# A second buffer for raw MLP weights, a later MLP residual, and attention's residual made ahead of the scan

## The chip, the cores and the metric

The kernel runs on one core of one Trainium2 chip. The metric is the device time of one execution in microseconds (us); a lower time is better. The core has TensorE (PE in the profile, with its weight loads as PEld), VectorE (DVE), ScalarE (ACT), GpSimd (POOL) and SyncE (SP, which here only issues transfers).

## What is computed

One encoder layer over 1024 tokens of width 1024, in float32. The input is normalised, projected, and split into two head groups: four heads of a bidirectional gated DeltaNet (a chunked scan) and eight heads of neighbourhood attention. Their outputs are mixed by one projection; residual and LayerNorm follow, then a squared-ReLU MLP with residual and LayerNorm.

```python
x = layer_norm(x, ln_in_g, ln_in_b)
h = x @ w_in
o_gdn = gdn_mixer(...)                      # scan, both directions
o_na = rms_norm(neighborhood_attention(...))
mix = concat(o_gdn, o_na) @ w_out
x = layer_norm(ALPHA * x + mix, ln1_g, ln1_b)
ff = relu(x @ w1 + b1) ** 2
x = layer_norm(ALPHA * x + ff @ w2 + b2, ln2_g, ln2_b)
```

## The kernel before, in words

**Precision.** Every large operand is split into a high and a low part of type float32r: ScalarE copies the high part, and `sub_split` (line 71) subtracts it on another engine for the low part. A product takes three matmuls for each 128-row block.

**Order of work.** The program is written in Tile. A planner reads the whole program, allots the buffers of each tag, and puts every engine's instructions, and SP's and ACT's transfers, into one fixed order per engine: of the instructions whose inputs and buffers its own simulation holds to be ready, the one that comes first in the program goes first. So a transfer may be issued well ahead of its place in the text, as soon as its buffer is free. `tc.issue_after(ins)` holds an instruction behind another one, and `pacer` spreads matmuls of one kind behind anchors of another. On the chip each engine then works through its list in order, and an instruction that waits holds up all that stand behind it.

**Stages, in order of time.**
- Projection, convolution and the triangular inverse of the DeltaNet (lines 173 to 512), up to about 330 us. `inverse(b)` (lines 296 to 391) is one long chain on DVE (lines 311 to 317), a round trip through DRAM, and small matmuls with copies on ACT and DVE. The pool `p1` (from line 196) holds, among others, the tags `hraw` (2 buffers) and `cy` (3 buffers) of the convolution.
- The scan (lines 543 to 614), with the matmuls of attention's projections (`na_v`, `na_qk`) as filler between its steps. Its pool `p2` takes over space of `p1`, tile by tile.
- Attention (lines 719 to 765) in four passes `p` of two heads, 16 tiles of scores each, with parts of the output projection as filler: `units[p]` (line 820) says which. `out_proj` (line 792) splits its left side on ACT and POOL, multiplies, and adds two 128x512 halves into `yacc[t]` on DVE (line 805). Units 0 to 7 are the DeltaNet half for the eight 128-token blocks t; units 8 to 15 are the first half of attention's heads; the rest follows after pass 3.
- The residual of attention is made in pass 0 (lines 816 to 831). Two broadcasts `xg`, `xb` of ln_in_g and ln_in_b are loaded and scaled by ALPHA on ACT; each block of x is loaded into `yacc[t]`, normalised on ACT, and multiplied and added on POOL:

```python
                with tc.issue_after(loads[2 + t // 4].ins):
                    D.dma_start(yacc[t], A["x"][t * P:(t + 1) * P, :])
                S.activation(yacc[t], yacc[t], AF.Identity, scale=rstd0[:, t:t + 1], bias=nmr0[:, t:t + 1])
                G.tensor_tensor(yacc[t], yacc[t], xg, ALU.mult)
                G.tensor_tensor(yacc[t], yacc[t], xb, ALU.add)
```

- POOL also makes the small `rsqrt` of attention (line 93, from line 763) and the low part `ol` of `out_proj`. DVE makes the row sums for it with three tiny 128x4 instructions (lines 760 to 762).
- The MLP's first layer (lines 853 to 1178) uses Strassen's seven products in place of eight for 16 groups `g`: `w_steps` makes sums of w1 in tiles `ws` (tag `tt`, 6 buffers, shared with six early weight tiles `w1q`), `up_pair` multiplies. Between them `w2_load` and `w2_sums` (lines 1023 to 1036) read w2 in pieces of 256 KB a transfer into `w2r` (one buffer) and store sums for the second layer in DRAM (`t_d`).
- The MLP's second layer (lines 1145 to 1299) runs 7 products x 4 groups, n = 0 to 27. `down_ops(n)` loads two raw operands (1 MB each, into `big` or `q8` buffers) and splits them on ACT and DVE; `down_ops(n + 2)` is called ahead of n's matmuls. `first_ops` (line 1171) calls it for n = 0 and 1 in the last `up_pair`. `take(0, ...)` after n = 3 is the first to need the MLP's residual `yr`. That is made ahead of the loop (lines 1183 to 1194): five broadcasts, eight loads of `y_d`, and 18 DVE instructions.

Of the kernel before, what the change touches and what calls it, by code (L numbers as in the profile page):

```python
# [7 lines left out]
F32 = mybir.dt.float32  # L8
F32R = mybir.dt.float32r
AF = mybir.ActivationFunctionType  # L10
ALU = mybir.AluOpType
# [4 lines left out]
P = 128  # L16
T = 1024
DM = 1024
NK = DM // P
NT = T // P  # L20
DFF = 4096
NF = DFF // P
ALPHA = 2.0 ** 0.25
# [13 lines left out]
def tile_trunk(ctx: ExitStack, tc: tile.TileContext, A: dict, out: bass.AP):  # L37
    nc = tc.nc
    V, S, G, TE, D = nc.vector, nc.scalar, nc.gpsimd, nc.tensor, nc.sync
# [35 lines left out]
    dr = open_pool("dram", space=DRAM)  # L75
# [13 lines left out]
    rstd0 = cp.tile([P, NT], F32, name="rstd0")  # L89
# [128 lines left out]
    vt_d = dr.tile([8, P, 4, P], F32, name="vt_d")  # L218
    qk_d = [dr.tile([8, P, 4, P], F32, name=f"qk_d{d}") for d in range(2)]
    z_d = dr.tile([4, P, T], F32, name="z_d")  # L220
    gc_d = dr.tile([2, 2, 32, P], F32, name="gc_d")

    AY = [bigp.tile([P, 32, P], F32, tag="big", name=f"AY{b}", bufs=2) for b in range(2)]
# [287 lines left out]
        gdn_chunk("v", h)  # L511
    inverse(0)
    inverse(1)

    rk = p1.tile([P, 32], F32, name="rk")
    rkp = p1.tile([P, 32], F32, name="rkp")
# [196 lines left out]
    loads = []  # L713
# [75 lines left out]
    def raw8():  # L789
        return op.tile([P, 2, DM], F32, tag="q8", name="wraw", bufs=2)  # L790

    def out_proj(t, oT, hi, lo, pool, tag, eng, pace=lambda mm: None, nb=2):
        nk = len(hi)
        oh = pool.tile([P, nk, P], F32R, tag="oh", name="oh", bufs=nb)
        ol = pool.tile([P, nk, P], F32R, tag="ol", name="ol", bufs=nb)
        S.activation(oh, oT, AF.Copy)
        sub_split(eng, ol, oT, oh)
        for half in range(2):
            c = slice(half * 512, half * 512 + 512)
            ps = psC.tile([P, 512], F32, tag=tag[half % len(tag)], name="psop", bufs=2)  # L800
            for k in range(nk):
                pace(TE.matmul(ps, oh[:, k], hi[k][:, c], start=(k == 0), stop=False))  # L802
                pace(TE.matmul(ps, oh[:, k], lo[k][:, c], start=False, stop=False))
                pace(TE.matmul(ps, ol[:, k], hi[k][:, c], start=False, stop=(k == nk - 1)))
            V.tensor_tensor(yacc[t][:, c], yacc[t][:, c], ps, ALU.add)

    pre["h", 0] = load_qk(0)
    pre["b", 0, 0] = load_b(0, 0)
# [4 lines left out]
    with tc.issue_after(kload[0].ins):  # L813
        pre["v", 1] = load_v(1)
    wo1 = None
    xg, xb = (p3.tile([P, DM], F32, name=x) for x in ("xg", "xb"))
    for t_, nm in ((xg, "ln_in_g"), (xb, "ln_in_b")):
        D.dma_start(t_, A[nm].to_broadcast([P, DM]))
        S.activation(t_, t_, AF.Copy, scale=ALPHA)
    units = ((0, 1, 2, 3), (4, 5), (6, 7, 8, 9), range(10, 16))  # L820
    first = (2, 0, 0, 0)
    late = (0, 0, 0, 24)
    for p in range(4):
        attention(p)
        if p == 0:
            for t in range(NT):
                with tc.issue_after(loads[2 + t // 4].ins):
                    D.dma_start(yacc[t], A["x"][t * P:(t + 1) * P, :])
                S.activation(yacc[t], yacc[t], AF.Identity, scale=rstd0[:, t:t + 1], bias=nmr0[:, t:t + 1])
                G.tensor_tensor(yacc[t], yacc[t], xg, ALU.mult)  # L830
                G.tensor_tensor(yacc[t], yacc[t], xb, ALU.add)
        anchors = tiles[p * 16 + first[p]:p * 16 + 16]
        nmm = sum(24 if u < 8 else 12 for u in units[p]) - late[p]
        pace = pacer(anchors, 0, nmm / len(anchors), True)
        for u in units[p]:
            if u == 8:
                r = [raw8() for i in range(2)]
                wo1 = load_wo(1, [r[k // 2][:, k % 2] for k in range(4)])
            t = u % 8
            if u < 8:  # L840
                out_proj(t, oaccs[t // 4][:, t % 4], *wo0, p3, "p", G, pace)
            else:
                out_proj(t, oTn[0][:, :, t * P:(t + 1) * P], wo1[0][0:2], wo1[1][0:2], p3, "p", G, pace)
        attention_out(p)
# [22 lines left out]
        X[nm] = bigp.tile([P, 2, 4, 512], F32R, tag="big", name="x" + nm, bufs=2)  # L867

    def tmp(name):
        return wk.tile([P, 512], F32, tag="tt", name=name, bufs=6)  # L870

    def hold8(name):
        return wk.tile([P, 512], F32, tag="f0", name=name, bufs=8)
# [147 lines left out]
    raws1[1] = w1_raw(1)  # L1021

    def w2_load(g, hc):
        r = w2p.tile([P, 2, 2, 256], F32, tag="r", name="w2r", bufs=1)
        for k in range(2):
            D.dma_start(r[:, k], A["w2"][(2 * g + k) * P:(2 * g + k + 1) * P, :]
                        .rearrange("p (j c) -> p j c", j=2)[:, :, hc * 256:hc * 256 + 256])
        return r
# [152 lines left out]

    fp = open_pool("fin")
    gB, bB, g2B, b2L, b2B = (fp.tile([P, DM], F32, name=x) for x in ("gB", "bB", "g2B", "b2L", "b2B"))
    for t_, nm in ((gB, "ln1_g"), (bB, "ln1_b"), (b2B, "b2"), (g2B, "ln2_g"), (b2L, "ln2_b")):
        D.dma_start(t_, A[nm].to_broadcast([P, DM]))
    V.tensor_scalar(gB, gB, ALPHA, None, ALU.mult)
    V.scalar_tensor_tensor(bB, bB, ALPHA, b2B, ALU.mult, ALU.add)
    yr = []
    for t in range(NT):
        y = yp.tile([P, DM], F32, tag="y", name="yr", bufs=8)  # L1190
        D.dma_start(y, y_d[t])
        V.tensor_tensor(y, y, gB, ALU.mult)
        V.tensor_tensor(y, y, bB, ALU.add)
        yr.append(y)
    us = [fp.tile([P, 512], F32, name=f"us{q}") for q in range(4)]
    sts = {}

# [73 lines left out]
    for i in range(7):  # L1271
# [7 lines left out]
        for gr in range(NQ):  # L1279
            n = i * NQ + gr  # L1280
            if n + 2 < 7 * NQ:
                down_ops(n + 2)
            if i == 6 and gr >= NQ - 2:
                continue
            for q in range(4):
# [96 lines left out]
```

## Time and profile before

| what | value |
|---|---|
| time, median of 3 runs | 1384.3 us |
| lowest and highest of the runs | 1372.8 and 1384.89 us |
| the profiled execution's own time | 1387.8 us |
| span in its profile (first to last instruction) | 1385.8 us |
| mean granted TensorE clock | 0.977 |
| bytes moved by transfers | 268.32 MB |

The profile is of one execution. The span is what its rows divide; 2.0 us of the execution's time lie outside. The engines' busy shares are means over stages with different limits. In the rows, "[x <-E L]" is how long the engine had been idle ahead of an instruction and which instruction of which engine ended that; "x8" after a name is a count.

### The profile page before, as it was taken

The numbers are of one execution on the slowest core, as the hardware profiler recorded it, in microseconds if no ns is written. First come the engines' busy times: TensorE is split into PE (matmuls) and PEld (weight loads), VectorE is DVE, ScalarE is ACT, GpSimd is POOL, SyncE is SP. The second block draws the span as 40 slices with busy tenths as digits, with TensorE's granted clock in tenths as the row PEclk, the third lists the DMA queues.
The fourth block names the chain that finished last, engine by engine and source line by source line (L and its number), as shares of the span: only waits on it lengthen the run. The fifth ranks groups of instructions, "written<-read, shape, count | busy, mean of one in ns | idle before, by whom it ended". The sixth has DMA issues, their size and how long they took to land. (4 is left out here: it accounts for less than half of the span.)

```text
span 1385.8 us, 20027 instructions
## 1 busy us (share of the span) xinstructions
PE 1293.7 (93%) x7318; PEld 1072.5 (77%) x7318; DVE 947.9 (68%) x1707; ACT 634.3 (46%) x1224; POOL 187.8 (14%) x208
## 2 busy tenths in 40 slices
PE   5999999999999977699998899999998999999996
PEld 4688888888888866688875687777786788888885
DVE  6755797942348645757699886777875686565855
ACT  5457666434333145346366454444444433333531
POOL 3000001011113237513130000000000000000403
PEclk9999999999999999899999899999999899999998
DMA  6134548466877599565154677677779957555721
GB/s 193 51 99 126 145 122 182 124 147 202 234 224 222 135 277 329 150 173 147 45 179 134 213 257 250 208 248 259 238 267 354 396 197 246 182 182 193 257 96 61
DMA packets 242690, 268.32 MB, mean 194 GB/s; under 512 B 38928, under 2 KB 171920, under 8 KB 242592
## 3 DMA queue, kind: packets, MB, share of 16 engines
q1 hardware_dynamic: 208416, 216.70, 51.8%
q10 hardware_dynamic: 34176, 50.34, 10.4%
q8 instruction: 58, 0.95, 0.3%
q14 instruction: 40, 0.33, 0.1%
HBM read 181.99 MB, written 85.00 MB: 193 GB/s over the span
## 5 line engine op out<-in xcount | busy, mean ns | idle before, releaser
L1266 PE MATMUL psdn<-d,d 128*128 128x512 f32 (+1 forms) x464 | 175.3, 386 | 6.9 <-ACT d L1166 6.9
L1267 PE MATMUL psdn<-d,d 128*128 128x512 f32 (+1 forms) x464 | 177.9, 384 | 0.1
L1268 PE MATMUL psdn<-d,d 128*128 128x512 f32 (+1 forms) x464 | 177.6, 383 | 0.0
L71 DVE TENSOR_TENSOR d<-d2r,d 128x1024 fp32r<-128x1024 f32 x72 | 85.6, 1239 | 63.4 <-ACT d L1166 63.4
L1166 ACT ACTIVATE d<-d2r 128x1024 fp32r<-128x1024 f32 x72 | 71.3, 1048 | 109.5 <-PE psdn L1268 91.1
L1266 PEld LDWEIGHTS psdn<-d,d 128*128 128x128 f32 x464 | 88.0, 190 | 24.7 <-ACT d L1166 7.8
L1267 PEld LDWEIGHTS psdn<-d,d 128*128 128x128 f32 x464 | 87.8, 189 | 17.7 <-DVE d L71 0.6
L1268 PEld LDWEIGHTS psdn<-d,d 128*128 128x128 f32 x464 | 87.8, 189 | 17.2
L93 POOL TENSOR_TENSOR lrs<-lrs,mhalf 128x1 f32<-128x1 f32 x8 | 6.4, 806 | 615.5 <-DVE lrs L1208 615.5
L120 PE MATMUL psj<-xlo,whi 128*128 128x512 f32 x192 | 77.4, 403 | 1.9 <-DVE xlo L71 1.9
L119 PE MATMUL psj<-xhi,whi 128*128 128x512 f32 x192 | 77.0, 402 | 0.7 <-DVE xhi L170 0.7
L121 PE MATMUL psj<-xhi,wlo 128*128 128x512 f32 x192 | 76.5, 398 | 0.0
L71 DVE TENSOR_TENSOR d<-wraw,d 128x1024 fp32r<-128x1024 f32 x40 | 47.9, 1236 | 30.1 <-ACT d L1166 30.1
L1039 ACT ACTIVATE h<-h,b1T 128x512 f32<-128x512 f32 x48 | 34.7, 722 | 73.9 <-DVE h L1105 37.6
L71 DVE TENSOR_TENSOR wlo<-wraw,whi 128x1024 fp32r<-128x1024 f32 x28 | 34.3, 1223 | 47.9 <-ACT whi L110 43.3
L883 ACT ACTIVATE w1t<-ws 128x512 fp32r<-128x512 f32 x64 | 39.9, 626 | 57.9 <-DVE hs L1137 17.0
L1166 ACT ACTIVATE d<-wraw 128x1024 fp32r<-128x1024 f32 x40 | 40.0, 1049 | 55.1 <-PE psdn L1268 44.9
L240 DVE SCALAR_TENSOR_TENSOR cy<-hraw,convw,cy 128x1024 f32<-128x1024 f32 x48 | 61.2, 1281 | 5.6 <-ACT cy L238 4.5
L754 PEld LDWEIGHTS po<-vt,et 128*128 128x128 f32 x384 | 51.3, 194 | 7.9 <-ACT et L752 3.7
L743 ACT ACTIVATE ex<-sn,nm 128x384 f32<-128x384 f32 x64 | 39.0, 610 | 36.0 <-DVE nm L739 20.5
L754 PE MATMUL po<-vt,et 128*128 128x64 f32 x384 | 50.7, 271 | 4.4 <-ACT et L752 2.9
L802 PE MATMUL psop<-wo,oh 128*128 128x512 f32 x128 | 52.9, 416 | 1.6 <-ACT wo L785 1.3
(340 smaller groups left out, 3488.8 us busy)
## 6 DMA issues: line engine op xcount, KB each, us to landing
wraw<-in_w_dram SPq DMA_DIRECT2D x21, 1024.0 KB, 7.3
d2r<-h_d SPq DMA_DIRECT2D x18, 1024.0 KB, 5.5
w2r<-in_w_dram SPq DMA_DIRECT2D x64, 256.0 KB, 4.8
t_d<-w2s ACTq DMA_DIRECT2D x32, 512.0 KB, 4.8
h_d<-hs ACTq DMA_DIRECT2D x64, 256.0 KB, 2.1
wraw<-in_w_in_dram SPq DMA_DIRECT2D x28, 512.0 KB, 4.5
h_d<-h ACTq DMA_DIRECT2D x48, 256.0 KB, 5.3
d2r<-t_d SPq DMA_DIRECT2D x11, 1024.0 KB, 9.3
```

The source lines that it names most:

```text
L71: return eng.tensor_tensor(lo, full, f32(hi), ALU.subtract)
L119: pace(TE.matmul(ps, hi[:, kt], xhi[:, kt, sl], start=(kt == 0), stop=False))
L120: pace(TE.matmul(ps, hi[:, kt], xlo[:, kt, sl], start=False, stop=False))
L121: pace(TE.matmul(ps, lo[:, kt], xhi[:, kt, sl], start=False, stop=(kt == NK - 1)))
L240: V.scalar_tensor_tensor(y, raw[:, i:i + T], convw[:, ci, i:i + 1], y, ALU.mult, ALU.add)
L754: mm = TE.matmul(po[:, j], et[:, c], vts[j][:, t + c, e * 64:e * 64 + 64], start=(c == 0), stop=(c == 2))
L802: pace(TE.matmul(ps, oh[:, k], hi[k][:, c], start=(k == 0), stop=False))
L883: S.activation(t[:, 0], src, AF.Copy)
L1166: S.activation(t[:, 0, k], raw[:, k], AF.Copy)
L1266: TE.matmul(ps, h[:, 0, k, qs_], w[:, 0, k, c], start=(start and k == 0), stop=False)
L1267: TE.matmul(ps, h[:, 0, k, qs_], w[:, 1, k, c], start=False, stop=False)
L1268: TE.matmul(ps, h[:, 1, k, qs_], w[:, 0, k, c], start=False, stop=(stop and k == 3))
```

## The change

1. Attention's residual is made after the two `inverse` calls and ahead of the scan, in tiles of the tags `hraw` (`xg`, `xb`) and `cy` (`xs`): load, normalise on ACT, multiply and add on DVE, store to a DRAM tile `xr_d`. In attention the first `out_proj` of each block writes `yacc[t]` by two ACT copies instead of adding on DVE, and a transfer issued by POOL adds `xr_d[t]` to it in place.
2. `w2r` has two buffers; the tag `tt` has four instead of six.
3. The MLP's residual is made from n = 1 of the second layer's loop, behind the call of `down_ops(3)`, with three broadcasts; the other two (`g2B`, `b2L`) are loaded at n = 8. Its tiles `yr` are still allotted ahead of the loop.

```diff
+    xr_d = dr.tile([NT, P, DM], F32, name="xr_d")
...
     inverse(1)
+    xg, xb = (p1.tile([P, T + 4], F32, tag="hraw", name="xgb", bufs=2)[:, 0:DM] for i in range(2))
+    for t_, nm in ((xg, "ln_in_g"), (xb, "ln_in_b")):
+        D.dma_start(t_, A[nm].to_broadcast([P, DM]))
+        S.activation(t_, t_, AF.Copy, scale=ALPHA)
+    for t in range(NT):
+        xs = p1.tile([P, T], F32, tag="cy", name="xs", bufs=3)
+        D.dma_start(xs, A["x"][t * P:(t + 1) * P, :])
+        S.activation(xs, xs, AF.Identity, scale=rstd0[:, t:t + 1], bias=nmr0[:, t:t + 1])
+        V.tensor_tensor(xs, xs, xg, ALU.mult)
+        V.tensor_tensor(xs, xs, xb, ALU.add)
+        D.dma_start(xr_d[t], xs)
...
-            V.tensor_tensor(yacc[t][:, c], yacc[t][:, c], ps, ALU.add)
+            if first:
+                S.activation(yacc[t][:, c], ps, AF.Copy)
+            else:
+                V.tensor_tensor(yacc[t][:, c], yacc[t][:, c], ps, ALU.add)
...
-    xg, xb = (p3.tile([P, DM], F32, name=x) for x in ("xg", "xb"))
-    for t_, nm in ((xg, "ln_in_g"), (xb, "ln_in_b")):
-        D.dma_start(t_, A[nm].to_broadcast([P, DM]))
-        S.activation(t_, t_, AF.Copy, scale=ALPHA)
...
-        if p == 0:
-            for t in range(NT):
-                with tc.issue_after(loads[2 + t // 4].ins):
-                    D.dma_start(yacc[t], A["x"][t * P:(t + 1) * P, :])
-                S.activation(yacc[t], yacc[t], AF.Identity, scale=rstd0[:, t:t + 1], bias=nmr0[:, t:t + 1])
-                G.tensor_tensor(yacc[t], yacc[t], xg, ALU.mult)
-                G.tensor_tensor(yacc[t], yacc[t], xb, ALU.add)
...
-                out_proj(t, oaccs[t // 4][:, t % 4], *wo0, p3, "p", G, pace)
+                out_proj(t, oaccs[t // 4][:, t % 4], *wo0, p3, "p", G, pace, first=True)
+                G.dma_start(yacc[t], xr_d[t], accum_op=ALU.add)
...
-        return wk.tile([P, 512], F32, tag="tt", name=name, bufs=6)
+        return wk.tile([P, 512], F32, tag="tt", name=name, bufs=4)
...
-        r = w2p.tile([P, 2, 2, 256], F32, tag="r", name="w2r", bufs=1)
+        r = w2p.tile([P, 2, 2, 256], F32, tag="r", name="w2r", bufs=2)
...
-    for t_, nm in ((gB, "ln1_g"), (bB, "ln1_b"), (b2B, "b2"), (g2B, "ln2_g"), (b2L, "ln2_b")):
-        D.dma_start(t_, A[nm].to_broadcast([P, DM]))
...
-    for t in range(NT):
-        y = yp.tile([P, DM], F32, tag="y", name="yr", bufs=8)
-        D.dma_start(y, y_d[t])
...
+    yr = [yp.tile([P, DM], F32, tag="y", name="yr", bufs=8) for t in range(NT)]
+    def residual():
+        for t_, nm in ((gB, "ln1_g"), (bB, "ln1_b"), (b2B, "b2")):
+            D.dma_start(t_, A[nm].to_broadcast([P, DM]))
+        V.tensor_scalar(gB, gB, ALPHA, None, ALU.mult)
+        V.scalar_tensor_tensor(bB, bB, ALPHA, b2B, ALU.mult, ALU.add)
+        for t, y in enumerate(yr):
+            D.dma_start(y, y_d[t])
+            V.tensor_tensor(y, y, gB, ALU.mult)
+            V.tensor_tensor(y, y, bB, ALU.add)
...
             if n + 2 < 7 * NQ:
                 down_ops(n + 2)
+            if n == 1:
+                residual()
+            if n == 8:
+                for t_, nm in ((g2B, "ln2_g"), (b2L, "ln2_b")):
+                    D.dma_start(t_, A[nm].to_broadcast([P, DM]))
```

## Rows read from the trace of the kernel before

**Rows 1.** The page: busy time by engine, and PE's in 40 slices.

```profile
PE 1293.7 (93%) x7318; PEld 1072.5 (77%) x7318; DVE 947.9 (68%) x1707; ACT 634.3 (46%) x1224; POOL 187.8 (14%) x208
PE   5999999999999977699998899999998999999996
```

**Rows 2.** Stretches of 20 us: busy PE, PEld, DVE, ACT, POOL, PEclk, DMA share, GB/s.

```profile
500.00:520.00 20.00, 12.65 (x78) 10.33 (x76) 9.45 (x17) 8.92 (x18) 8.92 (x5) 1.00 1.01 276
520.00:540.00 20.00, 12.94 (x77) 11.91 (x78) 12.62 (x26) 16.54 (x30) 10.82 (x5) 0.83 1.03 360
540.00:560.00 20.00, 12.94 (x65) 10.28 (x64) 13.58 (x10) 3.13 (x6) 20.00 (x10) 0.91 0.98 243
560.00:580.00 20.00, 14.63 (x78) 12.71 (x79) 16.68 (x33) 8.35 (x24) 11.94 (x8) 0.75 0.39 108
580.00:600.00 20.00, 20.00 (x134) 18.24 (x133) 9.12 (x27) 7.71 (x19) 3.58 (x3) 1.00 0.56 161
```

**Rows 3.** Timeline of PE in the first attention pass.

```profile
524.56 0.69 PE L735 MATMUL pss<-kk,qs 128*128 128x384 f32 x1 [7.26 <-DVE nm L739]
...
564.54 0.69 PE L735 MATMUL pss<-kk,qs 128*128 128x384 f32 x1 [10.79 <-DVE nm L739]
```

**Rows 4.** DVE's groups by form, 500 to 580 us: busy us, mean ns.

```profile
L762 DVE SCALAR_TENSOR_TENSOR rs<-rs,sums 128x4 f32<-128x4 f32 x5 | 12.9, 2584 | 0.1
...
L761 DVE TENSOR_SCALAR sums<-sums 128x4 f32<-128x4 f32 x5 | 8.8, 1754 | 0.1
L760 DVE TENSOR_TENSOR sums<-sums 128x4 f32<-128x4 f32 x5 | 6.2, 1245 | 1.6 <-ACT ex L743 1.6
```

**Rows 5.** Timeline of DVE in the same pass.

```profile
523.94 0.56 DVE L739 CUSTOM_DVE_ANT_0 sn<-pss,B 128x384 f32<-128x384 f32 x1 [5.35 <-DMA B<-in_rpbT_dram]
...
552.71 11.30 DVE L762 SCALAR_TENSOR_TENSOR rs<-rs,sums 128x4 f32<-128x4 f32 x1
...
577.29 0.16 DVE L761 TENSOR_SCALAR sums<-sums 128x4 f32<-128x4 f32 x1
```

**Rows 6.** Timeline of POOL beside it.

```profile
551.23 4.65 POOL L830 TENSOR_TENSOR yacc<-yacc,xg 128x1024 f32<-128x1024 f32 x2
```

**Rows 7.** The tile yacc: durations min/median/max in ns, first and last start.

```profile
L828 SPq DMA_DIRECT2D yacc<-in_x_dram x8: 327/400/1116, 517.8 to 525.4; - x8
L829 ACT ACTIVATE yacc<-yacc,nmr,rstd x8: 1230/1236/1247, 527.9 to 539.8; 128x1024 f32<-128x1024 f32 x8
L830 POOL TENSOR_TENSOR yacc<-yacc,xg x8: 2331/2370/2391, 529.2 to 553.5; 128x1024 f32<-128x1024 f32 x8
L831 POOL TENSOR_TENSOR yacc<-yacc,xb x8: 2331/2353/2406, 533.8 to 569.4; 128x1024 f32<-128x1024 f32 x8
```

**Rows 8.** Timeline of SP's issues ahead of pass 0's second head.

```profile
513.95 2.30 SPq L818 DMA_DIRECT2D xg<-in_ln_in_g_dram  x1
...
516.82 0.91 SPq L709 DMA_DIRECT2D B<-in_rpbT_dram  x2
```

**Rows 9.** One stretch around the second inverse, columns as in rows 2.

```profile
255.00:335.00 80.00, 76.82 (x1261) 64.42 (x1260) 41.68 (x81) 30.77 (x50) 12.21 (x19) 0.96 0.61 149
```

**Rows 10.** The page's groups: a 128x1024 two-input DVE instruction.

```profile
L71 DVE TENSOR_TENSOR wlo<-wraw,whi 128x1024 fp32r<-128x1024 f32 x28 | 34.3, 1223 | 47.9 <-ACT whi L110 43.3
```

**Rows 11.** ACT's groups by form, 1100 to 1120 us: a 128x512 PSUM copy.

```profile
L1241 ACT ACTIVATE us<-psdn 128x512 f32<-128x512 f32 x4 | 2.4, 594 | 4.0 <-PE psdn L1268 4.0
```

**Rows 12.** Waits in the first MLP layer, 784 to 1060 us: total, times, longest.

```profile
PE psF L925 <- DVE u L1101: 9.0, 9, 2.1
...
DVE w2s L1032 <- DMA w2r<-in_w_dram: 14.2, 11, 2.7
```

**Rows 13.** Between the MLP's layers: SP's timeline.

```profile
1043.02 9.51 SPq L1191 DMA_DIRECT2D yr<-y_d  x5
...
1058.83 0.42 SPq L1163 DMA_DIRECT2D d2r<-h_d  x1
```

**Rows 14.** Between the MLP's layers: PE's timeline.

```profile
1075.89 2.07 PE L1266 MATMUL psdn<-d,d 128*128 128x512 f32 x4 [6.67 <-ACT d L1166]
```

More of the change, by code (lines that the diff above doesn't have):

```diff
@@ L790, in raw8, with out_proj @@
         return op.tile([P, 2, DM], F32, tag="q8", name="wraw", bufs=2)
-    def out_proj(t, oT, hi, lo, pool, tag, eng, pace=lambda mm: None, nb=2):
+    def out_proj(t, oT, hi, lo, pool, tag, eng, pace=lambda mm: None, nb=2, first=False):
         nk = len(hi)
@@ L1183, in tile_trunk @@
     gB, bB, g2B, b2L, b2B = (fp.tile([P, DM], F32, name=x) for x in ("gB", "bB", "g2B", "b2L", "b2B"))
-    for t_, nm in ((gB, "ln1_g"), (bB, "ln1_b"), (b2B, "b2"), (g2B, "ln2_g"), (b2L, "ln2_b")):
-        D.dma_start(t_, A[nm].to_broadcast([P, DM]))
-    V.tensor_scalar(gB, gB, ALPHA, None, ALU.mult)
-    V.scalar_tensor_tensor(bB, bB, ALPHA, b2B, ALU.mult, ALU.add)
-    yr = []
-    for t in range(NT):
-        y = yp.tile([P, DM], F32, tag="y", name="yr", bufs=8)
-        D.dma_start(y, y_d[t])
-        V.tensor_tensor(y, y, gB, ALU.mult)
-        V.tensor_tensor(y, y, bB, ALU.add)
-        yr.append(y)
+    yr = [yp.tile([P, DM], F32, tag="y", name="yr", bufs=8) for t in range(NT)]
[8 more added lines that the diff above has]
+            V.tensor_tensor(y, y, bB, ALU.add)
     us = [fp.tile([P, 512], F32, name=f"us{q}") for q in range(4)]
```

## The prediction

> **What bounds the kernel now.** I read the page first: PE is busy for 93% of the span [rows 1], so most of the kernel is matmul time that this change does not touch, and the most that any edit can win is PE's idle time and the time spent at a lower clock. The 40 slices say where that is: three slices stand at 7, 7 and 6 tenths in the middle, where attention starts, and single 8s stand in and behind the MLP's first layer [rows 1]. So I cut the middle into stretches of 20 us. From 500 to 580 us PE is busy 12.65 + 12.94 + 12.94 + 14.63 = 53.16 of 80 us, 26.8 us idle, with a granted clock of 0.83, 0.91 and 0.75 in the last three; the stretch behind it is full again [rows 2]. The transfers' share is about 1 for the first three, and POOL is busy for all of 540 to 560 [rows 2].
>
> PE's timeline there has two long gaps, 7.26 and 10.79 us, both ended by line 739 on DVE [rows 3]. DVE's timeline tells them apart. In the first, DVE itself waited for a bias tile B [rows 5]. In the second it waited for nothing: a 128x4 instruction of line 762 lasted 11.30 us [rows 5], while POOL ran its two-input instructions back to back [rows 6]. It is not a single accident: in this stretch the three tiny instructions of lines 760 to 762, 15 in all, took 6.2 + 8.8 + 12.9 = 27.9 us [rows 4]; one that nothing disturbs takes 0.16 [rows 5]. So some 27.9 - 15 x 0.16 = 25.5 us of DVE are lost to POOL's residual pass, whose 16 instructions of about 2.36 us [rows 7] make 37.8 us of POOL.
>
> The Trainium skill has a rule for this (page "SBUF — State Buffer", section "SBUF: two separate sides"): DVE with two SBUF inputs and GpSimd share one port pair, an exclusive lock held for one instruction. By that rule alone a tiny instruction would wait for one POOL instruction, 2.4 us, and the second gap would be some 2 us. The trace has 11.30, across several POOL instructions in a row, and I go by that.
>
> **The change, part by part.** The sum is made against the profiled execution, 1387.8 us. It lies 3.5 us above the median of the runs, 1384.3, and I take those 3.5 off at the end.
>
> *Attention, what goes.* The 16 POOL instructions, 8 ACT instructions of 1.236 us, 8 loads of x (4.2 MB) and the two broadcasts leave the stretch [rows 7, 8].
> - The gap of 10.79 us [rows 3] has no other cause in sight: -10.8.
> - The gap of 7.26 [rows 3] ends with B. B's issue at 516.82 stands right behind the two broadcasts, whose issues begin at 513.95 [rows 8]: 2.9 us earlier. B is not the only transfer under way, so I take -3 of the 7.26, between 0 and -7.
> - The rest of the 26.8 us idle, 8.8, is made of waits of about a us. The other blocked DVE instructions (25.5 - 11.1 = 14.4 us of DVE) are behind a part of them: -3.
> - Clock: 0.17 + 0.09 + 0.25 of 20 us each [rows 2] is 10.2 us if PE had been busy throughout, so some 7 at its real share. It fell in the stretches that hold the gaps. With one gap gone and the other halved: -4.
>
> *Attention, what comes.* 16 copies of a PSUM half on ACT, 0.594 each [rows 11], 9.5 us, against the 9.9 us of ACT that go with the x tiles, so ACT is no busier; 16 additions leave DVE. Then 8 accumulating transfers from POOL's queue. No row shows one. Behind each stand POOL's next `ol` and `rsqrt`, and behind those PE's low products and the row norms. From below, 0: POOL gives up 37.8 us and has room. From above, POOL needs for an issue as long as the longest of SP's, 2.30 us [rows 8], and each delays PE: 8 x 2.3 = 18. POOL is nearly idle once the pass is gone, so I am near the lower end: +1. Their data are first needed at unit 8, in pass 2.
>
> Attention together: -10.8 - 3 - 3 - 4 + 1 = -20, between -5 and -33.
>
> *Ahead of the scan.* Added: 16 DVE instructions of about 1.22 us [rows 10], 19.5 us; 8 ACT instructions of 1.236 [rows 7] and two scalings, some 12 us; 18 SP issues, with 4.2 MB in, 4.2 MB out and two broadcasts. Around the second inverse, 255 to 335 us, DVE has 80 - 41.7 = 38 us free, ACT 49, and the transfers 0.39 x 80 = 31 us [rows 9]; 9.4 MB at the 276 GB/s of a full stretch [rows 2] are 34 us. So the engines have room; the transfers just. DVE's own chain of the inverse runs there too, and an `xs` instruction put between two of its links makes it 1.2 us longer; an SP store that waits for DVE holds up the filler's weights behind it. PE is busy for 76.8 of the 80 [rows 9] and full during the scan (slices 10 to 13 are 9s, [rows 1]), so a scan that starts some us later is covered as long as the filler has its weights. Bounds: 0, and 19.5 if all of DVE's work delays PE. I take +4.
>
> *`w2r` doubled, `tt` cut.* DVE waited 14.2 us for `w2r` from 784 to 1060, but PE's named wait there is only 9.0, for DVE [rows 12]. Doubling lets SP go on to w1's loads, too. Of the 9.0 I take -3. The four buffers of `tt` make the fifth and sixth `w1q` load wait for the first splits, and hold the sums of the next group back; at worst that gives the 3 back and as much again. Bounds -9 and +4.
>
> *The later residual.* After the first layer PE stands for 6.67 us [rows 14] while ACT waits for the raw operands of n = 1, 1 MB each, issued at 1058.83 behind the `y_d` loads of 1043.02 [rows 13]. If those 4.2 MB were truly later, the gap and the slow start behind it would go. But these rows also show that the planner had issued loads ahead of n = 1's though they stand behind them in the program: it issues a load once its buffer is free. The change moves the loads in the text, not the point where the buffers of `yr` come free, and puts no `issue_after` on them. I expect them at the same place: 0. DVE's 18 residual instructions have PE's matmuls of n = 1 to 3 as cover, and did not stop them before.
>
> Sum: -20 + 4 - 3 + 0 = -19, so 1368.8 on the profiled execution's scale and 1365 on the median's.
>
> **The rivals.**
> *A: the later residual is really later.* For it: the call stands behind `down_ops(3)`, and a different order of SP may keep the loads back. Against it: the rows above. Then the 6.67 us go, and about 3 us of slow clock behind them: 1365 - 9.7 = 1355.
> *B: attention's start stays bound by transfers.* For it: the share is 1.01, 1.03 and 0.98 [rows 2]. The bytes come back as accumulating transfers; then only the gap made by POOL goes with some 2 us of its clock: -10.8 - 2 + 4 + 1 - 3.5 = -11.3, so 1376.5. Against it: the first gap's transfer was issued late, and after 560 the share is 0.39 and 0.56 [rows 2], which is where most of them fall. (The Trainium skill speaks for this rival: by page "DMA: Bandwidth & Descriptors", section "Issuing engines are not separate DMA queues", a transfer from GpSimd runs on the same 16 engines as the others. No row here shows one from GpSimd.)
> *C, slower: the residual's pass ahead of the scan delays the scan beyond its cover.* One mechanism: `xs` tiles turn over in 3 buffers, and each needs a load, ACT, twice DVE and a store before it is free; with a load of 10 us (from the issues of 517.8 to ACT's start at 527.9 [rows 7]), 1.24, 2.44 and a store taken at under half of that load, 4, a tile holds its buffer for 18 us, and 8 tiles through 3 buffers need 47 us. If the scan's first tiles lie on these buffers and PE's filler runs out, 40 us of that stand in the open: 1387.8 + 40 - 23 - 3.5 = 1401. It is slower than before from a front delay of 23 us on. Against it: PE is full through the scan, so the filler isn't all needed.
>
> **How the numbers follow.** The forecast has 0.55, A 0.20, B 0.16, C 0.09. The forecast's own range is 1352 to 1379, from the bounds of the clock (0 to -7), of B's gap and of the front (0 to 12). The range for 8 in 10 takes in A with the larger win in the first layer, 1340, and reaches past B towards C, 1387. Within 1%, 13.8 us, is about what a measurement of this kernel can't tell from no change, so faster means under 1370.5: 0.70 of the forecast, 0.9 of A and 0.25 of B, 0.385 + 0.18 + 0.04 = 0.60. Slower, over 1398, is most of C and a tail: 0.08. Same: 0.32.
>
> **What would show it.** Right: lines 760 to 762 at 0.16 us each, no PE gap over 5 us in attention's first pass behind B's, and attention's end some 20 us earlier against the scan's end. The `y_d` loads are issued ahead of n = 1's operands again and PE stands for about 6 us there. Wrong: PE gaps between 290 and 340 us of over 5 us, or a later scan with PE idle in it (C); B's wait as long as before and transfers at 1 up to 560 (B); POOL's issues of several us each with PE waiting for `ol`.

## The result, and the profile after

The kernel after takes 1374.1 us (median of 20 runs, 1367.8 to 1377.0); before, run beside it, takes 1382.3 (20 runs, 1371.3 to 1390.5). The ratio is 0.9947, 95% interval 0.9927 to 0.9966. So the change wins about 8 us; forecast were 19, with a range that holds the result.

Three marks on PE cut the profiled executions: the first score matmul of attention, the first transpose of `yacc` (the end of attention and of its projection), and the last matmul of the second MLP layer (the start of line 1266's last one, 1272 in after).

| stretch | before | after | difference | forecast |
|---|---|---|---|---|
| start to the first score matmul | 492.6 | 520.0 | +27.4 | +4 |
| from there to the first transpose of `yacc` | 203.4 | 178.6 | -24.8 | -20 |
| from there to the last second-layer matmul | 677.5 | 663.2 | -14.3 | -3 |
| sum | 1373.5 | 1361.8 | -11.7 | -19 |

The mechanisms forecast for attention came about; the first stretch was mis-sized by 23 us, and the third gained five times what was forecast.

The page of after, PE's busy time and its 40 slices [rows 1]:

```profile
PE 1302.6 (95%) x7318; PEld 1082.6 (79%) x7318; DVE 931.2 (68%) x1707; ACT 644.2 (47%) x1240; POOL 155.6 (11%) x200
...
PE   5999999889999998999999799999998999999996
```

The hole at attention's start, 7, 7 and 6 before, is down to one 8 (slice 16); the 7 that is left is slice 23, ahead of the MLP. But two 8s stand in slices 8 and 9 (240 to 309 us), where there were none. The stretches of after, columns as in [rows 2]:

```profile
260.00:280.00 20.00, 14.88 (x175) 12.62 (x176) 16.24 (x23) 9.32 (x12) 2.07 (x4) 0.78 0.77 215
280.00:300.00 20.00, 15.51 (x312) 12.55 (x311) 16.72 (x28) 6.95 (x9) 0.41 (x1) 0.84 0.78 253
300.00:320.00 20.00, 20.00 (x174) 16.25 (x173) 17.10 (x32) 11.35 (x17) 3.50 (x5) 0.96 0.82 251
320.00:340.00 20.00, 16.92 (x243) 13.86 (x243) 1.70 (x3) 3.50 (x6) 2.07 (x4) 0.90 0.79 153
340.00:360.00 20.00, 20.00 (x309) 17.48 (x306) 4.05 (x6) 5.66 (x10) 2.08 (x4) 0.59 0.23 55
...
520.00:540.00 20.00, 15.53 (x82) 13.08 (x81) 12.11 (x28) 12.76 (x28) 7.68 (x5) 0.83 1.05 314
540.00:560.00 20.00, 20.00 (x118) 17.52 (x117) 7.31 (x25) 8.52 (x22) 6.06 (x6) 1.00 1.11 270
560.00:580.00 20.00, 18.49 (x121) 16.10 (x119) 6.15 (x22) 10.41 (x26) 6.35 (x6) 1.00 1.08 293
```

Multiply PE's busy time by its clock: from 260 to 360 us that makes, as an estimate, 11.6 + 13.0 + 19.2 + 15.2 + 11.8 = 70.8 us of full-speed work in 100. Of the 29.2 us lost, 12.7 are idle time and 16.5 the granted clock, which is 0.59 in the last of these stretches (most of it at 1.2 in place of 2.4 GHz, behind a stretch with 3 us of idle PE). The same stretches of before:

```profile
260.00:280.00 20.00, 19.38 (x334) 16.35 (x335) 19.25 (x38) 7.10 (x11) 2.07 (x4) 1.00 0.57 146
280.00:300.00 20.00, 20.00 (x282) 16.29 (x280) 10.29 (x25) 6.87 (x11) 2.09 (x4) 1.00 0.69 146
300.00:320.00 20.00, 17.56 (x477) 15.48 (x477) 4.58 (x6) 7.20 (x12) 4.08 (x6) 0.85 0.56 121
320.00:340.00 20.00, 19.94 (x173) 16.75 (x172) 3.82 (x6) 9.53 (x20) 5.01 (x7) 0.98 0.82 261
340.00:360.00 20.00, 20.00 (x119) 17.63 (x118) 4.20 (x9) 8.50 (x19) 1.04 (x1) 1.00 0.93 269
```

They make 19.4 + 20 + 14.9 + 19.5 + 20 = 93.8, with 3.1 us idle and 3.0 of clock. After loses 23 us more here, most of the first stretch's 27.4.

Why PE runs dry there is seen on DVE, after's timeline in the second inverse (lines 316 and 318 are the links of the chain, 523 and 524 the residual's pass):

```profile
277.12 0.42 DVE L316 TENSOR_TENSOR itmp<-iab,iX 128x255 f32<-128x255 f32 x1
279.80 1.22 DVE L523 TENSOR_TENSOR xs<-xs,xgb 128x1024 f32<-128x1024 f32 x1 [2.25 <-ACT xs L522]
280.94 0.42 DVE L318 TENSOR_TENSOR iX<-iX,itmp 128x255 f32<-128x255 f32 x1
...
286.65 0.41 DVE L316 TENSOR_TENSOR itmp<-iab,iX 128x240 f32<-128x240 f32 x1
289.98 1.22 DVE L523 TENSOR_TENSOR xs<-xs,xgb 128x1024 f32<-128x1024 f32 x1 [2.91 <-ACT xs L522]
291.12 0.40 DVE L318 TENSOR_TENSOR iX<-iX,itmp 128x240 f32<-128x240 f32 x1
```

Two links that would stand 0.45 us apart are 3.8 and 4.5 us apart: an instruction of the pass stands between them, and DVE, which takes its list in order, idles until ACT has normalised that block. ACT itself waits for the loads of x, after's waits of ACT from 240 to 330 us (total, times, longest):

```profile
ACT xs L522 <- DMA xs<-in_x_dram: 21.0, 6, 7.8
```

The inverse's last DVE instruction starts at 316.4 in place of 287.0 us. The tile of it in after (first and last start; one for each inverse):

```profile
L320 DVE COPY iXt<-iX x2: 1089/1143/1197, 210.6 to 316.4; 128x1024 f32<-128x1024 f32 x2
```

In attention the tiny instructions are nearly what they should be (0.16, 0.17 and, for line 774, 0.47 us on average); after's groups on DVE from 500 to 580 us (the first pass begins at 520) [rows 4]:

```profile
L774 DVE SCALAR_TENSOR_TENSOR rs<-rs,sums 128x4 f32<-128x4 f32 x4 | 1.9, 472 | 0.1
...
L772 DVE TENSOR_TENSOR sums<-sums 128x4 f32<-128x4 f32 x5 | 0.8, 159 | 0.2 <-ACT ex L755 0.2
L773 DVE TENSOR_SCALAR sums<-sums 128x4 f32<-128x4 f32 x4 | 0.7, 173 | 0.0
```

These 13 take 3.4 us where 15 took 27.9. PE's waits in after from 520 to 600 us have none over 2.5:

```profile
PE pss L747 <- DVE nm L751: 2.8, 3, 1.4
PE po L766 <- ACT et L764: 2.5, 1, 2.5
```

And the accumulating transfers, after's tile `yacc`, durations of an issue on POOL and the time to landing:

```profile
L846 POOL DMA_DIRECT2D yacc<-xr_d x8: 894/910/1057, 547.1 to 645.1; - x8
...
DMA to landing us min/median/max: 2.6/6.2/11.3
```

### The profile page after: what moved, and what is told of

Same layout as the page of the kernel before. It is cut to its first block, busy times and chain, and to the rows that moved or that the text cites. A ratio compares the mean times of both kernels' runs of the same rounds, so it can differ in the third digit from the quotient of the medians.

```text
span 1374.2 us, 20107 instructions
## 1 busy us (share of the span) xinstructions
PE 1302.6 (95%) x7318; PEld 1082.6 (79%) x7318; DVE 931.2 (68%) x1707; ACT 644.2 (47%) x1240; POOL 155.6 (11%) x200
## 5 line engine op out<-in xcount | busy, mean ns | idle before, releaser
L1171 ACT ACTIVATE d<-d2r 128x1024 fp32r<-128x1024 f32 x72 | 71.3, 1048 | 114.3 <-PE psdn L1274 92.9
L119 PE MATMUL psn<-xhi,whi 128*128 128x512 f32 x128 | 53.6, 419 | 0.0
```

Of the source, the lines that this page charges most:

```text
L119: pace(TE.matmul(ps, hi[:, kt], xhi[:, kt, sl], start=(kt == 0), stop=False))
L1171: S.activation(t[:, 0, k], raw[:, k], AF.Copy)
```

## The experiments

All are medians with the ratio to the kernel before, run beside them; the marks are of the profiled execution.

| kernel | us | ratio, 95% | inverse's last DVE | first score | first transpose | last matmul |
|---|---|---|---|---|---|---|
| before, profile ahead | | | 287.0 | 492.6 | 696.0 | 1373.5 |
| before, second profile (`e15_again`) | 1383.4 | 0.997 to 1.004 | 285.7 | 492.1 | 692.9 | 1368.5 |
| after | 1374.1 | 0.993 to 0.997 | 316.4 | 520.0 | 698.6 | 1361.8 |
| part 1 alone (`e12_part1`) | 1388.2 | 1.003 to 1.010 | 313.0 | 515.6 | 694.3 | 1372.1 |
| part 2 alone (`e1_w2r`) | 1365.8 | 0.985 to 0.994 | 285.1 | 489.9 | 684.9 | 1346.0 |
| `tt` cut alone (`e13_tt4`) | 1366.1 | 0.987 to 0.994 | 286.5 | 491.7 | 692.5 | 1354.3 |
| part 3 alone (`e6_resid`) | 1376.2 | 0.995 to 1.003 | 286.5 | 491.7 | 683.6 | 1359.8 |
| after without the pass (`e2_nofront`) | 1348.1 | 0.972 to 0.979 | 286.4 | 492.8 | 672.2 | 1334.0 |
| pass behind the chain (`e3_held`) | 1358.9 | 0.981 to 0.987 | 287.9 | 501.1 | 682.4 | 1341.3 |
| pass without loads (`e5_nowait`) | 1367.4 | 0.986 to 0.994 | 309.8 | 506.8 | 686.7 | 1352.4 |
| pass in the scan (`e7_scan`) | 1359.4 | 0.980 to 0.987 | 286.2 | 501.6 | 680.4 | 1342.0 |
| pass early (`e10_early`) | 1345.7 | 0.971 to 0.981 | 298.3 | 492.7 | 672.2 | 1338.9 |
| before, residual on DVE (`e4_dve`) | 1372.8 | 0.992 to 0.997 | 286.2 | 492.6 | 681.4 | 1358.9 |
| that with part 2 (`e8_combo`) | 1358.7 | 0.980 to 0.987 | 288.0 | 494.0 | 681.9 | 1346.7 |
| `y_d` loads held (`e9_late`) | 1380.7 | 0.996 to 1.001 | 314.4 | 519.2 | 702.0 | 1374.0 |
| pass early, stores by POOL (`e11_pool`) | 1350.3 | 0.973 to 0.982 | 294.7 | 489.6 | 672.1 | 1336.1 |

### The three parts by themselves

**Part 1 alone**, the kernel before with the pass, the ACT copies and the accumulating transfers.

> The kernel before with part 1 alone: residual's pass ahead of the scan, first halves copied by ACT, POOL's accumulating transfers. If the parts add (part 2 alone -15.6 by its median, the whole change -8), part 1 by itself is a loss of some 4 to 8 us or nothing: 1382 to 1390. The prediction had -16 for it: 1366.

1388.2 us: slower than before by 0.3 to 1.0%. Attention takes 178.7 us, as in after, but starts at 515.6.

**Part 2 alone.**

```diff
-        return wk.tile([P, 512], F32, tag="tt", name=name, bufs=6)
+        return wk.tile([P, 512], F32, tag="tt", name=name, bufs=4)
...
-        r = w2p.tile([P, 2, 2, 256], F32, tag="r", name="w2r", bufs=1)
+        r = w2p.tile([P, 2, 2, 256], F32, tag="r", name="w2r", bufs=2)
```

> The kernel before with part 2 alone: two buffers for w2r, four for tt. The reading of the two traces (first to last copy of u in the first MLP layer: 285.7 us before, 271.8 after) says that part 2 alone gives about -14 us there and, the rest being as before, about 1370 against 1382.3. The rival is the prediction's own size of -3 (1379), with the other 11 us of the first layer coming from something else that changed, such as another order of the plan behind attention.

-15.6 us against the median beside it; the six runs lie in two groups, 1359.4 to 1360.4 and 1371.2 to 1372.5. From the first transpose to the last matmul it takes 661.1 us, against 677.5 and 675.6 in the two profiles of before. So part 2 makes all that after wins, and more.

**Part 3 alone.**

> The kernel before with part 3 alone: the MLP's residual called from n = 1, two broadcasts at n = 8. The prediction and the rows of after (the y_d loads still stand ahead of n = 1's operands, PE still stands for 6.4 us) say 0: 1382, within 5. The rival A would give -9.7: 1373.

No difference can be told (0.995 to 1.003); its third stretch is 676.2 us, as before.

The three together: +0.7%, -1.1%, -0.1%, so -0.5%, which is what after shows.

### Which half of part 2 does it

I took the second buffer of `w2r` for the cause and the cut of `tt` for its price. Here is the cut by itself.

> The kernel before with tt cut from six buffers to four, w2r left at one. If w2r's second buffer makes part 2's gain, the cut alone gives nothing or a loss: first MLP layer (first to last copy of u) at 285 us or more, time 1380 to 1390. If the other order of w1q's loads that the cut brings makes it, the first layer is at about 272 us and the time about 1368.

The expectation built on `w2r` fell: the cut alone has 1366.1 us, as part 2 whole, and 661.8 us in the third stretch. The second buffer adds nothing to the time that these runs can tell; no run has it alone. The other half of the expectation came out in part: from the first to the last copy of `u` the cut alone takes 277.0 us, not 272 (before 285.7 and, in its second profile, 284.0; part 2 whole 274.5). So about 8 of the 14 us lie in the first layer; most of the others lie at the start of the second, where PE's stall is 1.51 us in place of 6.67 and 5.53. The waits name the reason for the first layer's part. DVE and PE in the second profile of before, 780 to 1040 us (total, times, longest):

```profile
DVE ws L904 <- DMA wraw<-in_w_dram: 27.7, 12, 5.5
DVE w2s L1032 <- DMA w2r<-in_w_dram: 13.6, 10, 2.8
...
PE psF L925 <- DVE u L1101: 6.1, 5, 2.2
```

The same with the cut alone:

```profile
DVE w2s L1032 <- DMA w2r<-in_w_dram: 20.6, 15, 3.0
...
DVE ws L904 <- DMA wraw<-in_w_dram: 0.7, 1, 0.7
...
PE psF L925 <- DVE u L1101: 1.2, 3, 0.6
```

With six buffers DVE waited 27.7 us at the head of its list for w1's load `wraw`, with `u`, for which PE waits, queued behind the sums `ws`. With four that wait is gone, and PE's with it; DVE waits more for `w2r` (20.6), and PE does not feel it. I read this as the place of `ws` in the list: with fewer buffers it can't be put so early that its load is still under way. The waits show the effect; the planner's choice itself is argued.

The size has a lesson, too: PE's named wait was 9.0 us [rows 12] and went to 1.2, but it is not all that was lost there. Three stretches of the kernel before, columns as in [rows 2]:

```profile
820.00:840.00 20.00, 20.00 (x89) 16.41 (x88) 13.68 (x25) 8.59 (x15) 0.00 (x0) 1.00 0.69 230
840.00:860.00 20.00, 18.82 (x83) 15.12 (x82) 15.85 (x31) 10.13 (x18) 0.00 (x0) 1.00 0.70 231
860.00:880.00 20.00, 18.01 (x73) 14.26 (x72) 15.57 (x29) 7.33 (x14) 0.00 (x0) 0.91 0.69 223
```

A full stretch has 89 matmuls of this size (the first of the three). 73 of 89 are 82% of the work, where 18.01 of 20 us are 90% of the time: ends of matmuls are modelled, and the clock was 0.91. The count is the better measure.

### What the pass ahead of the scan costs

**Without it**, the transfers in attention add x itself, so normalisation and ALPHA are left out of the residual:

```diff
-                G.dma_start(yacc[t], xr_d[t], accum_op=ALU.add)
+                G.dma_start(yacc[t], A["x"][t * P:(t + 1) * P, :], accum_op=ALU.add)
```

> The kernel after without its pass ahead of the scan: POOL's accumulating transfers add x itself, so the residual's normalisation and scaling by ALPHA are left out; the transfers in attention stay the same in number and size. If the pass costs what the front's rows say (first score matmul at 520.0 us after, 492.6 before), attention starts at about 493 and the time is about 25 us under that of after: 1349. If the delay is absorbed by later cover, as the prediction's +4 had it, attention starts earlier but the end is at about 1370.

1348.1, as the front's rows said: the pass costs 26 us of the end, not 4.

**Behind the chain.** Its DVE instructions are held behind the inverse's last one.

```diff
+        with tc.issue_after(inv_end[1]):
             V.tensor_tensor(xs, xs, xg, ALU.mult)
             V.tensor_tensor(xs, xs, xb, ALU.add)
```

> The kernel after with its 16 DVE instructions of the pass held behind the last DVE instruction of the second inverse. Theory one (DVE's order: the pass stands between the links of the inverse's chain): the inverse's last DVE instruction is back from 316 at about 287 us, the scan starts at about 335 to 345, and the time is 10 to 25 us under that of after, 1350 to 1364. Theory two (the pass's transfers and the buffers that it holds keep the scan back): the inverse ends early but the scan's first loads still wait until the xs tiles are stored, and the scan starts at about 365 as in after: 1374.

The inverse is back at 287.9 and 15 us are won. But the first matmul of the scan's `psW` still comes at 355.3 (337.3 before), the first score at 501.1. So theory one holds for the larger part, and something of theory two for the rest: in this run PE stood 6.18 us for the inverse's own tile to come back from DRAM.

```profile
316.96 0.23 PE L363 MATMUL py<-ips,Xd 32*32 32x32 f32 x1 [6.18 <-DMA Xd<-dX]
```

**Without the loads of x** and ACT's part, DVE's instructions and the stores kept (x is then missing in the residual):

```diff
-        D.dma_start(xs, A["x"][t * P:(t + 1) * P, :])
-        S.activation(xs, xs, AF.Identity, scale=rstd0[:, t:t + 1], bias=nmr0[:, t:t + 1])
-        V.tensor_tensor(xs, xs, xg, ALU.mult)
+        V.tensor_tensor(xs, xb, xg, ALU.mult)
```

> The kernel after with its pass ahead of the scan kept at 16 DVE instructions of the same size and 8 stores, but without the loads of x and ACT's normalisation: xs is xg times xb, plus xb, so x is left out of the residual. It divides the front's 29 us (inverse's last DVE instruction 287.0 to 316.4). If DVE's own time does it, the inverse still ends at 287 + 19.5 = about 306 and the time is within 10 us of that of after: 1364 to 1374. If the waits in order do it (an xs instruction at the head of DVE's list that waits for a load or for ACT, with the next link behind it), the inverse ends at under 297 and most of the 25 us come back: about 1350 to 1358.

The inverse ends at 309.8: of the delay of 29.4 us, 22.8 stay, near DVE's own 19.5, and 6.6 were the waits in order. In the pass DVE waits only once here, for 0.45 us. But attention starts at 506.8, 13.2 us earlier than in after, so of its delay of 27.4 us about half goes with the loads and ACT's part. Both theories of the expectation are a part: DVE's own time is the larger at the inverse's end, and at attention's start they are about equal.

**In the scan**, in halves of 512 columns and a pool of its own.

> The kernel after with the pass moved behind the scan's text, in tiles of a pool of its own that lives through the scan (halves of 512 columns, four xs tiles of 2 KB a partition), so that no buffer of the inverse or of the scan waits for it. If the pass costs only through the inverse's chain and the buffers it shares, it is now nearly free: inverse's end at 287, the scan's first psW at 337 as before, attention's start at about 493, time about 1349, as with the pass left out. If DVE's order is what hurts anywhere, its 32 instructions of about 0.65 us and their waits now stand between the scan's links, and the scan ends 10 to 20 us later: 1359 to 1369.

The inverse and the scan's start are as before (286.2; first `psW` at 336.4), yet attention starts 9 us late, and the time is at the upper expectation, 1359.4. PE has 17.66, 16.16 and 19.02 us in the three stretches from 360, with transfers at 0.98, 0.92 and 1.00. Whether DVE's list or the transfers do that is not told apart here.

**Early**, behind the first head's projections, in tiles that the inverse doesn't need yet.

```diff
+        if h == 0:
+            xr_pass()
...
+        xgb = p1.tile([P, 32, 64], F32, tag="Xd", name="xgb").rearrange("p i j -> p (i j)")
...
+            xs = p1.tile([P, 32, 32], F32, tag=("iab", "iX")[t % 2], name="xs").rearrange("p i j -> p (i j)")
```

> The kernel after with its pass moved up, to where DVE has room and PE's queue is full (80 to 160 us): the text stands behind the first head's z_chunk, xg and xb lie in the tile of the inverse's Xd, the xs tiles in the inverse's iab and iX, all unused before the first inverse. If only the place of the pass is wrong, it is free there: inverse's end at 287, attention's start at 493, time 1348 to 1352, as with the pass left out. If 16 DVE instructions and 9 MB cost something wherever they stand, attention starts at 500 or later as in the two other placements, and the time is about 1359.

1345.7 us: 2.4% under before, 28 us under after, and within the scatter of the kernel that has no pass at all. The same instructions and bytes cost nothing that the time shows when they stand from 58 to 128 us: in before PE is busy throughout from 60 to 140 us, and DVE for 8.6 to 15.3 of each 20 us. This kernel's stretches where PE was dry in after:

```profile
260.00:280.00 20.00, 18.02 (x307) 14.99 (x305) 16.71 (x36) 4.87 (x7) 2.07 (x4) 0.74 0.46 109
280.00:300.00 20.00, 20.00 (x302) 16.49 (x289) 17.24 (x41) 8.64 (x14) 2.41 (x4) 1.00 0.36 94
300.00:320.00 20.00, 19.54 (x353) 16.05 (x353) 3.90 (x5) 5.81 (x9) 4.34 (x6) 1.00 0.89 183
320.00:340.00 20.00, 20.00 (x313) 16.48 (x312) 4.49 (x7) 7.93 (x13) 2.09 (x4) 1.00 0.45 109
340.00:360.00 20.00, 20.00 (x106) 17.13 (x105) 5.57 (x6) 9.81 (x22) 4.16 (x4) 1.00 1.01 341
```

By the same product as above, 13.3 + 20 + 19.5 + 20 + 20 = 92.9 of 100 us against 70.8. It also shows what cover the scan has: the inverse ends 11.3 us late (298.3) and the first `psW` 9 (346.4), but attention starts on time. So the cover that the prediction counted on is there, some 9 us of it. In after, the first `psW` was 35 us late and 27.4 remained.

### Attention: POOL's pass or the transfers

The smallest cure is the kernel before with the residual's 16 instructions on another engine.

```diff
-                G.tensor_tensor(yacc[t], yacc[t], xg, ALU.mult)
-                G.tensor_tensor(yacc[t], yacc[t], xb, ALU.add)
+                V.tensor_tensor(yacc[t], yacc[t], xg, ALU.mult)
+                V.tensor_tensor(yacc[t], yacc[t], xb, ALU.add)
```

> The kernel before with nothing changed but the engine of the residual's 16 multiplications and additions in attention: DVE in place of POOL. If POOL's two-input instructions are what stretched DVE's tiny ones (27.9 us for 15, one of them 11.30), these are back at about 0.16 us, the gap of 10.79 us goes, and DVE has 19.5 us of work more: about -10, 1372. If the wait for x's loads is what counts, DVE now stands in its order behind each x tile with the score tiles behind it, PE's gaps stay at 27 us or grow, and the time is that of before or more: 1382 to 1395.

1372.8, 0.5% under before, with 19.5 us more on DVE: the long waits of the tiny instructions are POOL's doing (the longest is 2.02 us here). Attention takes 188.8 us against 178.6 in after; the first pass keeps a PE gap of 5.29 us, in which DVE waited 3.38 us for B. What the tiny instructions waited for can be read from their ends: in before's first pass eight of them lasted over 1 us, and each ends 0.02 or 0.03 us behind an instruction of POOL. For seven it is the one that ran when they started. The eighth, of 11.30 us [rows 5], ends at 564.01, with the sixth POOL instruction in a row; POOL's timeline in before:

```profile
561.66 2.33 POOL L831 TENSOR_TENSOR yacc<-yacc,xb 128x1024 f32<-128x1024 f32 x1
```

With part 2 beside it:

> The kernel before with part 2 (two buffers for w2r, four for tt) and with attention's residual on DVE in place of POOL, no pass ahead of the scan. The two have shown -15.6 and -8.6 us by medians against 1381.4. If they lie in different stages they add: about 1357, which beats after without any round trip through DRAM. If the first layer's gain was partly the same run-to-run gain in attention (the run with part 2 alone had a shorter attention too), the sum falls short: about 1365.

The two add: 1358.7, under after, with no pass ahead of the scan and no round trip through DRAM.

**How firm is the gap of 10.79 us [rows 3]?** With no edit in attention, `e1_w2r` and `e6_resid` have the same order of instructions there as before, and 195.0 and 191.9 us in place of 203.4. PE's timeline in `e1_w2r` has 3.98 us where before had 10.79:

```profile
560.03 0.55 PE L735 MATMUL pss<-kk,qs 128*128 128x384 f32 x1 [3.98 <-DVE nm L739]
```

and in `e6_resid` PE is busy for 18.53 of the 20 us from 540 and 19.96 of the next 20. So the kernel before was profiled again.

> The kernel before, unchanged, profiled a second time. If the gap of 10.79 us makes the two groups of its runs, a profiled execution of about 1385 has a PE gap of 10 us near 554 us and about 203 us from the first score matmul to the first transpose of yacc, and one of about 1373 has a gap of under 5 us there and about 192. If something else makes them, the gap is there at either time.

Its twelve runs have a hole between 1377.2 and 1382.8 us: five under it (1372.6 to 1377.2), seven above (to 1389.1). In the 96 other runs of before beside the result and the experiments, 21 lie in that hole, 30 under it and 45 above, so the two groups overlap. The profiled one has 1382.8. Its PE and DVE timelines:

```profile
561.49 0.69 PE L735 MATMUL pss<-kk,qs 128*128 128x384 f32 x1 [8.97 <-DVE nm L739]
...
549.41 11.55 DVE L762 SCALAR_TENSOR_TENSOR rs<-rs,sums 128x4 f32<-128x4 f32 x1
```

An upper run has the gap (8.97, attention 200.8), and so had the first profile (1387.8 us) and that of `e13_tt4`, with the same order in attention (9.50 and 200.8, at 1368.4 among runs of 1362.5 to 1373.3). `e6_resid`, whose runs have the same hole (1371.5 to 1376.9, then 1386.6 and more), was profiled in its lower group, at 1374.4, without the gap. All agrees with the gap as the larger part of the difference between the groups; a lower run of before itself was not profiled, so this is not shown for it.

### Between the MLP's layers

**Really later loads.** The loads of `y_d` are held behind those of n = 2.

```diff
             if n == 1:
-                residual()
+                with tc.issue_after(ld2[2]):
+                    residual()
```

> The kernel after with the eight loads of y_d really held: behind the loads of n = 2 of the second layer. The prediction's rival A put the price of their early place at 9.7 us (6.67 us of PE idle and about 3 us of slow clock): then PE's stall at the start of the second layer goes and the time is about 10 us under that of after, 1364. The rival: n = 1's operands cannot come before their big buffers are free, whatever stands ahead of them, so the stall of about 6 us stays and the time with it: 1374.

Neither: 1380.7 us, 0.4% above after by the ratios, and PE's stall grew from 6.42 to 10.28 us. ACT's timeline here, from the first split of n = 1 to the second:

```profile
1059.67 2.01 ACT L1171 ACTIVATE d<-d2r 128x1024 fp32r<-128x1024 f32 x2 [1.46 <-DMA d2r<-h_d]
1062.59 13.51 ACTq L1147 DMA_DIRECT2D h_d<-hs  x2
1076.15 2.00 ACT L1171 ACTIVATE d<-d2r 128x1024 fp32r<-128x1024 f32 x2 [14.47 <-DMA d2r<-in_w_dram]
```

The trace puts the wait down to a load. But ACT's own issue of two stores runs from 1062.59 to 1076.10, and the split starts 0.05 us behind it. After has the same picture, smaller (its timelines of ACT and PE):

```profile
1060.21 4.34 ACTq L1147 DMA_DIRECT2D h_d<-hs  x3
1064.59 2.00 ACT L1171 ACTIVATE d<-d2r 128x1024 fp32r<-128x1024 f32 x2 [5.74 <-DMA wraw<-h_d]
...
1065.70 2.08 PE L1272 MATMUL psdn<-d,d 128*128 128x512 f32 x4 [6.42 <-ACT d L1171]
```

**The stores on POOL's queue** tells the two apart, on top of the early pass.

```diff
-            S.dma_start(h_d[3 + i, g], h)
+            (G if g == NG - 1 else S).dma_start(h_d[3 + i, g], h)
```

> The kernel with the early pass, and the four stores of hs to h_d of the last group issued by POOL, which is idle there, in place of ACT. In after ACT's issues of three of these took 4.34 us, and with the y_d loads bunched behind n = 2's loads two took 13.51 us, each time ending with the very split that PE waited 6.4 and 10.3 us for. If ACT's issue is what makes PE's stall at the start of the second layer, the stall is under 3 us and the time 3 to 6 us under that of the early pass. If the loads of n = 1's operands set it, the stall stays at about 6 us and the time is the same.

ACT's timeline has the second split 3.26 us behind the first, so its load had landed:

```profile
1031.50 2.01 ACT L1176 ACTIVATE d<-d2r 128x1024 fp32r<-128x1024 f32 x2 [1.34 <-DMA d2r<-h_d]
1034.76 2.01 ACT L1176 ACTIVATE d<-d2r 128x1024 fp32r<-128x1024 f32 x2 [1.25 <-DMA d2r<-in_w_dram]
```

PE's stall of 6.59 us at n = 1 in `e10_early` is gone; one of 3.40 comes 9 us later, for n = 2's operands, with transfers at 1.03. So ACT's issue of the stores made the stall at n = 1. What made the issue long is not told apart: the transfers' share was at 1.03, and in `e9_late` SP was issuing at the same time. The time is not better (1350.3 and 1345.7, with overlapping intervals), so the expected 3 to 6 us did not show.

## Why the prediction was right or wrong

**Ahead of the scan: +4 forecast, +27.4 measured.** This is the step that failed. The prediction named the mechanism ("an `xs` instruction put between two of its links makes it 1.2 us longer") and then weighed it by the engines' free time in one stretch of 80 us, 38 us of DVE [rows 9]. The mean hides where that time lies: while the chain runs, to 287 us, DVE is nearly full (19.25 of 20 us from 260), and almost all that is free lies behind the chain's end (4.58 and 3.82 of 20 from 300, in before's rows above). All 16 instructions stood ahead of that end, and in a list that is taken in order each lengthens the chain by its full time. That alone is the "upper bound" of 19.5. It was no bound, since an instruction that waits for its load holds the chain as well, another 6.6 us, and a thinner PE ran at a lower clock: 16.5 us against 3.0, a term that the sum has for attention and not here. The cover by the scan was real but 9 us.

The prediction's own sign of being wrong here, PE gaps of over 5 us between 290 and 340, did not come (the longest from 240 to 375 is 3.08); the later scan did. Rival C had a scan delayed beyond its cover, as it came, but not its time, 1401. Its mechanism, the turnover of three buffers, is not needed for the larger part of the inverse's delay (`e5_nowait`); for the waits for loads it is not ruled out.

**Attention: -20 forecast, -24.8 in the profiles.** Right in kind: lines 760 to 762 are back at 0.16 to 0.47 us, PE's longest wait in the first pass is 2.5 us though DVE still waits for B, POOL's issues cost it 0.91 us each. The size is for the profiled execution. The profile of before is one with the gap; without it the same order took 195.0 and 191.9 us (`e1_w2r`, `e6_resid`), and against these after wins 13 to 16. So an edit that takes the gap away wins less on the median; the prediction took only the profile's distance of 3.5 us off.

On the port that POOL and DVE share, the Trainium skill ("SBUF — State Buffer", "SBUF: two separate sides") has a lock held for one instruction. Seven of the eight long tiny instructions above agree with that, and `e4_dve` has none over 2.02 us. The eighth does not: it was shut out across six POOL instructions, and so was one of 11.55 us in the second profile of before. The pair of engines is as the page says; that one can be shut out several times in a row is the measurement's.

**`w2r` and `tt`: -3 forecast, -14 measured.** The sum credited the wrong half. The row on `w2r`, 14.2 us [rows 12], was matched with the edit that names `w2r`; the larger wait of the same view, DVE's for `wraw`, has no line in the diff, and the cut of `tt`, entered as a cost of up to 4, is what removed it. DVE's waits in before from 784 to 1060 us:

```profile
DVE ws L904 <- DMA wraw<-in_w_dram: 29.9, 12, 5.1
```

**The later residual: 0 forecast, 0 measured.** Right, by its own reason: the loads stayed ahead of n = 1's operands. Rival A's price, 9.7 us for loads that are truly later, has fallen too: they made the stall longer.

**B** (attention bound by transfers) is out: their share is 1.05 to 1.11 from 520 to 580 us, above before's, and PE is busy for 54 of those 60 us. Its time, 1376.5, also leaves out the -3 for `w2r` that the forecast has; with it the sum is 1373.5, near the measured 1374.1, but not by its mechanism. That the forecast's four terms hit the time to 9 us is luck: two errors of 23 and 11 us had opposite signs.

## What to carry to other kernels

A mean of free time over a long stretch does not say that the engine is free where the work will land. Here DVE's free time lay behind a dependent chain, and work put between the links cost its full length and its waits, since engines take their lists in order. Moved to where DVE had gaps and PE a full queue it cost nothing that the time shows (`e10_early`); that this is not enough everywhere is shown by `e7_scan`, 9 us late at attention's start. Time the parts of a change by themselves: here one part lost 7 us, and a cut that was meant as a price was the gain. Read a gap from more than one execution of the same code before you price it.

## What was not expected of the hardware

- Issuing a transfer can take an engine long. ACT issues one store in 0.33 us; with the transfers at a share of 1.03 two took 13.51, and SP's eight loads of `y_d` beside them 16.91, SP's timeline in `e9_late`:

```profile
1062.96 16.91 SPq L1197 DMA_DIRECT2D yr<-y_d  x8
```

  The Trainium skill ("DMA: Bandwidth & Descriptors", "Issuing engines are not separate DMA queues") has the time to initiate a transfer as usually small beside the transfer. Here it stopped ACT, and PE with it, for 10 us. The two long issues overlap, and ACT's end before SP's; whether the full transfers or the other engine's issues held them is not shown. With POOL issuing the stores the stall at n = 1 went, though the time did not fall.
- A tiny DVE instruction was held for 11.30, 11.55 and 10.64 us in three executions of the same order of attention (the third is `e13_tt4`), each to the end of the sixth POOL instruction in a row, and for at most 5.59 in two others.
- An accumulating transfer of 512 KB from POOL takes POOL 0.91 us (median) and lands after 2.6 to 11.3.
